# Two transformer blocks on one core: the router of the expert layer rebuilt, tokens gathered by pairs of experts in fp32, the output product finished block by block

## The chip, the cores and the metric

The kernel runs on one core of one Trainium2 chip. The metric is the device time of one execution in microseconds (us), as the median of several runs.

## The reference

256 tokens of width 1024 in fp32 go through two blocks. The first block has a mixer (gating over time beside a recurrence) and an expert layer, the second attention and a feed-forward part. The change lies at the end of the first block's mixer and in its expert layer:

```python
y = jnp.concatenate([y_a, y_b], axis=-1) @ w_out[l]          # the output product, 1024 x 1024
x = x + gate1[:, None, :] * y
h = _modulate(_rmsnorm(x, norm2_g[l]), shift2, scale2)
...
group_prob = jax.nn.softmax(ht @ rg_w + rg_b)                # 4 groups
g_p, g_idx = lax.top_k(group_prob, 1)
exp_logits = (ht @ re_w + re_b).reshape(N, 4, 8)             # 8 experts in each group
sel = jnp.take_along_axis(exp_logits, g_idx[:, :, None], axis=1)[:, 0]
e_p, e_idx = lax.top_k(jax.nn.softmax(sel, axis=-1), 2)
e_p = e_p / jnp.sum(e_p, axis=-1, keepdims=True)
weights = g_p * e_p
...
y_e = (silu(xb @ w_gate[e]) * (xb @ w_up[e])) @ w_down[e]    # for the tokens of each of 32 experts
```

Each token picks one group of four and two of its eight experts, whose results are added with their weights. The 32 experts have three matrices of 2 MiB each, 201 MB in all, and every one is read once. The shifts, scales and gates of a block come from a modulation, a product of one vector with a matrix of 1024 x 6144. The modulations of the second block do not depend on the first.

## The kernel before

**Order of work.** Most engines work in the order in which a scheduler places the instructions; inside `tc.manual_schedule` the order of the named engines is the order of the code. Loads are issued on SyncE's queue in the order of the code, and a load waits there until its buffer is free, with all that stand behind it.

**Output product** (`project_out`, from L845). For each of eight blocks of 128 weight rows the mixer's result is transposed and split in a high and a low part (`yh`, `yl`), the weight rows likewise by ACT (L167, `whi`) and VectorE (L168, `wlo`), in two buffers each. `mm3` (L416 to L418) then makes three products of 128x512 for each of two row tiles of tokens and two column halves, twelve per block, into four PSUM banks `pacc`. After the eighth block VectorE multiplies the four quarters by the gate and adds them to `x_sb`.

**Modulation** (L179 to L240). A vector of 1024 numbers takes four steps; a step loads 1 MiB, and makes eight small products per 128 rows (L190). The steps of the second block are used as filling: `fill(n)` places n of them, `need(...)` those that are still missing. `FILL_A[3]` = 8 steps stand ahead of the output product.

**Router** (from L948). Sixteen transposes of `x_sb` (L963), sixteen logit products of 36 columns (L971), the norm's factors, then the logits `L` for 4 groups and 32 experts. The group is chosen first (`first_max`: maximum, comparison, index, minimum, comparison), the eight logits of the chosen group are picked by multiplication and a sum (L1009), then the best and the second best of these, and their weights. `M` marks the two experts of a token. Products with a triangular matrix count the tokens of an expert ahead of each token, which gives its slot `pos`, and products with ones give the count of the fullest expert, `most`. The inputs for the experts are a scaled copy of `x_sb` as high and low part in fp32r: ACT writes `xh` (L1078) and `xf` (L1080), GpSimd `xl` (L1081).

**Experts** (L1187 to L1320). 16 pairs, in two groups (pairs 0 to 9 and 10 to 15), with PE's order by hand. `gather(quad)` compares slots with `pos` into a one-hot `D4` (L1190) and multiplies it with `xh` and `xl` (L1198): 32 products of 256 columns for four experts at 64 slots, copied to `xg` by ACT and VectorE in turn (L1202, L1204). `widen(j)` (L1216) makes the gate or the up product of a pair, 32 products of 512 columns, `narrow(j)` (L1261) the down product, `scatter(j)` (L1280, L1282) brings the results back to the tokens, with `x_sb` added after pair 12 (L1288). `places(j)` (L1240, L1245) turns the one-hot matrix. `turned(j)` transposes the hidden values. `bcast_cols` (L435) spreads a modulation vector over the partitions. Between the groups an `If` (L1120) treats experts with more than 64 tokens.

**Loads of the experts.** 192 loads of 1 MiB (`load_runs`, L149). The first 18 are issued ahead of the expert code, in the order `ORDER`, into buffers listed in `kept` (six of the ring shared with all loads of weights, `BIG` = 6 of the pool `bigp`, `MORE` = 2 of their own) and `EARLY` (buffers of tiles that are not in use yet). Each later one is issued when an earlier one's buffer is used up (`staged_moe`).

Of the kernel before, what the change touches and what calls it, by code (L numbers as in the profile page):

```python
# [20 lines left out]
D = 1024  # L21
# [38 lines left out]
def block(ctx, tc, A, out, dbg=None):  # L60
# [116 lines left out]
    on_dve = []  # L177

    def modulation(w, which, m, r0, each=False):  # L179
# [260 lines left out]
    with ExitStack() as c1:  # L440
# [404 lines left out]
        def project_out(kt):  # L845
# [16 lines left out]
            hi, lo = split_w(w_out[-1][:, kt % 2:kt % 2 + 1, :])  # L862
            for i in range(2):
                ts = slice(128 * i, 128 * i + 128)
                for n in range(2):
                    ns = slice(512 * n, 512 * n + 512)
                    mm3(op[i][n], (yh[:, kt, ts], yl[:, kt, ts]), (hi[:, 0, ns], lo[:, 0, ns]), kt == 0, kt == 7)
# [60 lines left out]
        for kt in range(4):  # L928
            project_out(kt)
# [6 lines left out]
        for kt in range(4, KT):  # L936
            project_out(kt)
        for i in range(2):
            for n in range(2):
                xs = x_sb[:, i, 512 * n:512 * n + 512]  # L940
                DVE.tensor_tensor(op[i][n], op[i][n], ga[:, n, :], op=OP.mult)
                DVE.tensor_tensor(xs, op[i][n], xs, op=OP.add)
        dump("x1", x_sb)


    with ExitStack() as c2:
        pool = c2.enter_context(tc.tile_pool(name="blk2", bufs=1, reuse_waits="tile"))
        G2 = pool.tile([128, 8], F32, name="G2")  # L948
        DVE.scalar_tensor_tensor(G2, modc[:, 4, :], 1.0, colr("n2g", 8), op0=OP.add, op1=OP.mult)
        big = lambda n: pool.tile([128, D], F32, name=n, tag="big", bufs=1)  # L950
        S2 = modc[:, 3, :]

# [6 lines left out]
        xT = pool.tile([128, KT, S], F32, name="xT", tag="xg", bufs=2)  # L959
        for kt in range(KT):  # L960
            p = pmm()
            for i in range(2):
                PE.transpose(p[:, 128 * i:128 * i + 128], x_sb[:, i, 128 * kt:128 * kt + 128], ident)  # L963
            if kt % 2:
                ACT.activation(xT[:, kt, :], p[:, 0:S], AF.Copy)
            else:
                DVE.tensor_copy(xT[:, kt, :], p[:, 0:S])
        pl = pmm()
        for i in range(2):
            for kt in range(KT):  # L970
                PE.matmul(pl[:, 64 * i:64 * i + 36], xT[:, kt, 128 * i:128 * i + 128], rw[:, kt, :],  # L971
                          start=i == 0 and kt == 0, stop=kt == KT - 1, skip_group_check=True)
        r = [rstd_x(i) for i in range(2)]
        need(5)
        need(6, 7)
        L = pool.tile([128, 2, 36], F32, name="L")
        for i in range(2):
            DVE.scalar_tensor_tensor(L[:, i, :], pl[:, 64 * i:64 * i + 36], r[i], rb, op0=OP.mult, op1=OP.add)


        t8 = lambda n, k=8: pool.tile([128, 2, k], F32, name="r_" + n)
        bb = lambda a, k: a.to_broadcast([128, 2, k])

        def first_max(v, k, n):

            m = t8(n + "m", 1)
            DVE.tensor_reduce(m, v, axis=AX.X, op=OP.max)
            c = t8(n + "c", k)
            DVE.tensor_tensor(c, v, bb(m, k), op=OP.is_equal)
            DVE.scalar_tensor_tensor(c, c, -64.0, io8[:, None, 0:k].to_broadcast([128, 2, k]), op0=OP.mult, op1=OP.add)  # L990
            f = t8(n + "f", 1)
            DVE.tensor_reduce(f, c, axis=AX.X, op=OP.min)
            o = t8(n + "o", k)
            DVE.tensor_tensor(o, c, bb(f, k), op=OP.is_equal)
            return m, o

        g4 = L[:, :, 0:4]
        gm_, og = first_max(g4, 4, "g")
        eg = t8("eg", 4)
        DVE.tensor_tensor(eg, g4, bb(gm_, 4), op=OP.subtract)  # L1000
        ACT.activation(eg, eg, AF.Exp)
        gs = t8("gs", 1)
        DVE.tensor_reduce(gs, eg, axis=AX.X, op=OP.add)
        pr = pool.tile([128, 2, 8, 4], F32, name="pr")
        for i in range(2):
            DVE.tensor_tensor(pr[:, i], L[:, i, 4:36].rearrange("p (g e) -> p e g", g=4),
                              og[:, i, None, :].to_broadcast([128, 8, 4]), op=OP.mult)
        sl8 = t8("sl8")
        DVE.tensor_reduce(sl8, pr, axis=AX.X, op=OP.add)  # L1009
        m1, o1 = first_max(sl8, 8, "a")  # L1010
        re8 = t8("re8")
        DVE.scalar_tensor_tensor(re8, o1, -1e30, sl8, op0=OP.mult, op1=OP.add)
        m2_, o2 = first_max(re8, 8, "b")
        e2 = t8("e2", 1)
        DVE.tensor_tensor(e2, m2_, m1, op=OP.subtract)
        ACT.activation(e2, e2, AF.Exp)
        w1, w2 = t8("w1", 1), t8("w2", 1)
        DVE.scalar_tensor_tensor(w1, e2, 1.0, gs, op0=OP.add, op1=OP.mult)
        DVE.reciprocal(w1, w1)
        DVE.tensor_tensor(w2, w1, e2, op=OP.mult)  # L1020
        M8, W8 = t8("M8"), t8("W8")
        DVE.tensor_tensor(M8, o1, o2, op=OP.add)
        DVE.tensor_tensor(o1, o1, bb(w1, 8), op=OP.mult)
        DVE.tensor_tensor(o2, o2, bb(w2, 8), op=OP.mult)
        DVE.tensor_tensor(W8, o1, o2, op=OP.add)
        M = pool.tile([128, 2, 32], F32, name="M")
        Wt = pool.tile([128, 2, 32], F32, name="Wt")
        for i in range(2):
            for dst, src in ((M, M8), (Wt, W8)):
                DVE.tensor_tensor(dst[:, i, :].rearrange("p (g e) -> p g e", g=4),  # L1030
                                  og[:, i, :, None].to_broadcast([128, 4, 8]),
                                  src[:, i, None, :].to_broadcast([128, 4, 8]), op=OP.mult)

        p = pmm()
        PE.matmul(p[:, 0:32], gt, M[:, 0, :], start=True, stop=True, skip_group_check=True)
        PE.matmul(p[:, 32:64], ones, M[:, 0, :], start=False, stop=False, skip_group_check=True)
        PE.matmul(p[:, 32:64], gt, M[:, 1, :], start=False, stop=True, skip_group_check=True)

        pc = pmm()
        PE.matmul(pc[:, 0:32], ones, M[:, 0, :], start=True, stop=False)  # L1040
# [68 lines left out]
        def crowded():  # L1109
# [10 lines left out]
            with tc.If(n_most > 64):  # L1120
                with tc.tile_pool(name="over", bufs=1) as op_, tc.For_i(0, 32) as e:
# [17 lines left out]
                    for b in range(2):  # L1139
                        bs = slice(128 * b, 128 * b + 128)  # L1140
                        p = pmm()
                        for i in range(2):
                            PE.matmul(p[:, 0:1], Do[:, i, bs].bitcast(F32), we_[:, i, :], start=i == 0, stop=i == 1)
# [610 lines left out]
```

## Time and profile before

| | us |
|---|---|
| median of 3 runs | 1443.49 (1443.27 to 1444.78) |
| the profiled execution's own time | 1445.49 |
| its span in the trace | 1443.7 |
| PE busy | 1356.1 (94%) |
| VectorE busy | 763.9 (53%) |
| ACT busy | 576.5 (40%) |
| GpSimd busy | 77.9 (5%) |

The DMA engines moved 400.42 MB, 277 GB/s in the mean. The page cuts the span in 40 slices of some 36 us:

```profile
PE   6999999699999988989979989999998999999997
...
PEclk9989999799999999999989999999999999999999
...
GB/s 361 295 69 251 164 274 380 226 365 426 426 427 426 427 427 402 391 426 427 427 246 252 196 228 146 336 276 311 286 248 181 172 117 149 184 196 196 178 150 30
```

Each digit is the busy share of PE in tenths, each PEclk digit TensorE's granted clock in tenths of full speed, the last line the DMA rate. Slice 7 (253 to 289 us, counted from 0) has the router: PE is busy for six tenths, at a clock of 0.7. The experts' loads fill slices 8 to 19. The busy shares are means over stages of different kinds; the rows further down are of single stretches and instructions.

### The profile page before, as it was taken

What the parts mean: (1) busy time and instruction counts of PE and PEld (TensorE: products, weight loads), DVE (VectorE), ACT (ScalarE), POOL (GpSimd) and SP (SyncE); (2) the same over time, 40 slices, a digit from 0 to 9 for tenths busy, and PEclk for the clock granted to TensorE, in tenths of its full rate; (3) what the DMA queues carried; (4) which work ended last, traced back from release to release, by engine and by line L of the source; (5) the groups of instructions that cost most, each with busy time, mean ns of one, the idle gap of its engine ahead of it and who ended that gap; (6) DMA issues with size and microseconds to landing.
All of it is one profiled execution on the core that took longest, in us unless ns stands there. A gap on an engine that the chain in (4) does not pass through costs nothing.

```text
span 1443.7 us, 22926 instructions
## 1 busy us (share of the span) xinstructions
PE 1356.1 (94%) x9330; PEld 1002.3 (69%) x9330; DVE 763.9 (53%) x1507; ACT 576.5 (40%) x1020; POOL 77.9 (5%) x79
## 2 busy tenths in 40 slices
PE   6999999699999988989979989999998999999997
PEld 5888878444444434534348867899996897799997
DVE  5648767511221111111165885888876575766565
ACT  3543013411111111101166755554456685654544
POOL 1002000100000000000020230000021001100000
PEclk9989999799999999999989999999999999999999
DMA  9826479599999999999967564988775534555540
GB/s 361 295 69 251 164 274 380 226 365 426 426 427 426 427 427 402 391 426 427 427 246 252 196 228 146 336 276 311 286 248 181 172 117 149 184 196 196 178 150 30
DMA packets 138688, 400.42 MB, mean 277 GB/s; under 512 B 6562, under 2 KB 84658, under 8 KB 114003
## 3 DMA queue, kind: packets, MB, share of 16 engines
q1 hardware_dynamic: 138578, 398.91, 72.0%
q8 instruction: 75, 1.23, 0.3%
q14 instruction: 35, 0.28, 0.1%
HBM read 397.82 MB, written 1.05 MB: 276 GB/s over the span
## 4 chain that ended last, share of the span: by engine, by line
PE 44%; DMA 9%; DVE 3%; ACT 3%; issue 1%; POOL 0%; POOLq 0%; DVEq 0%; SPq 0%; ACTq 0%
PE pmm L416 8%; PE pmm L417 8%; PE pmm L418 8%; PE pacc L416 5%; PE pacc L417 5%; PE pacc L418 5%; DMA wruns<-in_moe_w_gate_dram 4%; DMA wruns<-in_moe_w_down_dram 3%; DMA wruns<-in_moe_w_up_dram 2%; PE pmm L190 1%; PE pmm L1261 1%; ACT sqj L294 1%; PE pmm L366 1%; PE pmm L1622 1%; PE pmm L435 1%
## 5 line engine op out<-in xcount | busy, mean ns | idle before, releaser
L416 PE MATMUL pmm<-hh,whi 128*128 128x256 f32 (+1 forms) x1040 | 296.4, 285 | 2.0 <-ACT whi L167 2.0
L418 PE MATMUL pmm<-hh,wlo 128*128 128x256 f32 (+1 forms) x1040 | 297.1, 286 | 0.2 <-DVE wlo L168 0.2
L417 PE MATMUL pmm<-hl,whi 128*128 128x256 f32 (+1 forms) x1040 | 295.5, 284 | 0.0
L1216 PE MATMUL pmm<-wruns,xg 128*64 128x512 f32 x1024 | 233.1, 595 | 7.1 <-DMA wruns<-in_moe_w_gate_dram 7.1
L168 DVE TENSOR_TENSOR wlo<-wcols,whi 128x1024 fp32r<-128x1024 f32 (+1 forms) x130 | 168.4, 1300 | 99.3 <-ACT whi L167 98.8
L416 PEld LDWEIGHTS pmm<-hh,whi 128*128 128x128 f32 (+1 forms) x1040 | 197.6, 190 | 8.6 <-issue 3.6
L417 PEld LDWEIGHTS pmm<-hl,whi 128*128 128x128 f32 (+1 forms) x1040 | 196.6, 189 | 1.4
L418 PEld LDWEIGHTS pmm<-hh,wlo 128*128 128x128 f32 (+1 forms) x1040 | 197.0, 189 | 0.6 <-DVE wlo L168 0.4
L167 ACT ACTIVATE whi<-wcols 128x1024 fp32r<-128x1024 f32 (+1 forms) x130 | 136.1, 1053 | 119.0 <-PE pmm L417 91.7
L1216 PEld LDWEIGHTS pmm<-wruns,xg 128*64 128x64 f32 x1024 | 81.8, 137 | 141.1 <-issue 115.8
L168 DVE TENSOR_TENSOR wlo<-wrows,whi 128x1024 fp32r<-128x1024 f32 x87 | 108.1, 1248 | 56.3 <-ACT whi L167 55.9
L167 ACT ACTIVATE whi<-wrows 128x1024 fp32r<-128x1024 f32 x87 | 91.7, 1061 | 90.5 <-PE pmm L417 45.5
L1261 PE MATMUL pmm<-wruns,em 128*64 128x512 f32 x512 | 118.4, 595 | 7.2 <-DMA wruns<-in_moe_w_down_dram 5.7
L1261 PEld LDWEIGHTS pmm<-wruns,em 128*64 128x64 f32 x512 | 38.5, 137 | 79.3 <-issue 62.4
L1270 ACT ACTIVATE o<-ay 128x512 fp32r<-128x512 f32 x32 | 20.2, 631 | 177.5 <-DVE ay L1269 177.5
L1269 DVE SCALAR_TENSOR_TENSOR ay<-pmm,wsl,ga 128x512 f32<-128x512 f32 x32 | 24.0, 751 | 105.8 <-PE pmm L1261 103.8
L1307 DVE TENSOR_TENSOR ay<-ay,pmm 128x512 f32<-128x512 f32 x16 | 11.0, 688 | 120.0 <-PE pmm L1216 120.0
L1248 DVE COPY wsl<-pmm 64x1 f32<-64x1 f32 x32 | 5.0, 156 | 130.7 <-PE pmm L1245 130.4
L417 PE MATMUL pacc<-wlo,ah 128*128 128x512 f32 x176 | 69.2, 393 | 0.0
L416 PE MATMUL pacc<-whi,ah 128*128 128x512 f32 x176 | 68.9, 391 | 0.0
L418 PE MATMUL pacc<-whi,al 128*128 128x512 f32 x176 | 68.6, 393 | 0.0
L1222 ACT ACTIVATE ay<-pmm 128x512 f32<-128x512 f32 x16 | 9.6, 598 | 109.4 <-PE pmm L1216 109.4
(533 smaller groups left out, 2217.3 us busy)
## 6 DMA issues: line engine op xcount, KB each, us to landing
wruns<-in_moe_w_gate_dram SPq DMA_DIRECT2D x64, 1024.0 KB, 19.5
wruns<-in_moe_w_up_dram SPq DMA_DIRECT2D x64, 1024.0 KB, 19.5
wruns<-in_moe_w_down_dram SPq DMA_DIRECT2D x64, 1024.0 KB, 19.6
wrows<-in_w_mod_dram SPq DMA_DIRECT2D x48, 1024.0 KB, 7.0
wcols<-in_w_ffn_gate_dram SPq DMA_DIRECT2D x22, 1024.0 KB, 5.2
wcols<-in_w_ffn_up_dram SPq DMA_DIRECT2D x22, 1024.0 KB, 6.3
wrows<-in_w_ffn_down_dram SPq DMA_DIRECT2D x22, 1024.0 KB, 5.2
wrows<-in_ada_w_dram SPq DMA_DIRECT2D x16, 1024.0 KB, 7.7
```

Source lines behind the costliest of these rows:

```text
L167: ACT.activation(hi, src, AF.Copy)
L168: (POOL if ahead else DVE).tensor_tensor(lo, src, hi.bitcast(F32), op=OP.subtract)
L190: PE.matmul(p[32 * g:32 * g + 32, 0:n].rearrange("p (a j) -> p a j", j=32), lhsT, groups(rhs)[:, g], start=first, stop=last, skip_group_ch ...
L294: ACT.activation(j, src, AF.Square, accum_out=ss)
L366: PE.matmul(p, src[:, i, 128 * kt:128 * kt + 128], dg[i], start=True, stop=True)
L416: PE.matmul(p, a[0], b[0], start=first, stop=False, skip_group_check=True)
L417: PE.matmul(p, a[0], b[1], start=False, stop=False, skip_group_check=True)
L418: PE.matmul(p, a[1], b[0], start=False, stop=last, skip_group_check=True)
L1216: PE.matmul(p[64 * a:64 * a + 64, :], xg[:, kt, lc(2 * j + a)], wt[a][:, k, :], start=kt == 0, stop=kt == KT - 1, skip_group_check=True)
L1261: PE.matmul(pd[n][64 * a:64 * a + 64, :], hT[:, f, 64 * a:64 * a + 64], wt[a][:, b, 512 * n:512 * n + 512], start=f == 0, stop=f == 3, ski ...
L1269: DVE.scalar_tensor_tensor(yf, pd[n], wsl, ga2[:, ns], op0=OP.mult, op1=OP.mult)
L1270: ACT.activation(oh[:, ns], yf, AF.Copy)
```

## The change

- **Constants.** `MORE` 2 to 4; `ORDER` has load 18 in addition, `EARLY` no longer lends an `xg` buffer to load 12; `FILL_A[3]` 8 to 5.
- **Output product.** Blocks 0 to 5 as before. Blocks 6 and 7 are split first; then PE's, ACT's and VectorE's order is by hand: for each quarter (row tile, column half) the six products of both blocks, then its gate and sum, and for the first row tile the squares of the norm. Ahead of the last quarter PE transposes the first row tile (`turn_x`), four blocks into one PSUM bank. G2, the bias row `rb` and the scaling of `rw` move ahead of block 4.
- **Router.** PE's, VectorE's and ACT's order by hand. The logits of a row tile follow its transposes. Modulation steps stand at three places (`fill` 1, 2, 1), and in `hold` form: a vector's last three steps go into one PSUM bank and are added in one operation, after a further `yield`. The choice of best and second best is made in all four groups at once, on 8x8 elements per token partition (two row tiles by four groups), beside the group's choice; the product with the group's mark comes last. `M` is fp32r, and the products with it have fp32r copies of the triangle and of ones (`gtr`, `onr`). The weights `Wt` follow after the first one-hot matrix. The row factors for G2 and S2 are worked out ahead of the logits.
- **Gathering.** One scaled fp32 copy `xr` by ACT takes the place of `xh`, `xf` and `xl`; GpSimd's subtraction is gone. `gather(j)` is made for each pair instead of each second one: 16 fp32 products of 128 columns, into half of `xx`, the tile that held the transposes. It stands behind the up product of the pair before. `most` is worked out after the gathering for pair 1.

```diff
-MORE = 2
+MORE = 4
-EARLY = {4: "em", 3: "ay", 11: "oo", 12: "xg"}
-ORDER = (0, 1, 2, 5, 6, 7, 8, 9, 10, 3, 4, 11, 12, 13, 14, 15, 16, 17)
-FILL_A = (0, 0, 2, 8, 0, 2)
+EARLY = {4: "em", 3: "ay", 11: "oo"}
+ORDER = (0, 1, 2, 5, 6, 7, 8, 9, 10, 3, 4, 11, 12, 13, 14, 15, 16, 17, 18)
+FILL_A = (0, 0, 2, 5, 0, 2)
...
-                    p = gv[-1]()
+                    held = bool(hold) and q > 0
+                    if not held or q == 1:
+                        p = gv[-1]()
                     for kt in range(2 * q, 2 * q + 2):
-                        products(p, cb(kt), wt[:, kt % 2, :], kt == 2 * q, kt == 2 * q + 1)
-                    if q == 0:
+                        products(p, cb(kt), wt[:, kt % 2, :], kt == (2 if held else 2 * q), kt == (7 if held else 2 * q + 1))
+                    if held and q == 3:
+                        yield
+                    if held and q < 3:
+                        pass
+                    elif q == 0:
...
+        w = [project_out(kt) for kt in (6, 7)]
...
+        with tc.manual_schedule(engines={_E.PE, *MAN}):
+            for i in range(2):
+                for n, ns in enumerate(halves):
+                    for kt in (6, 7):
+                        project_on(kt, i, w[kt - 6], (n,))
+                    xs = x_sb[:, i, ns]
+                    DVE.tensor_tensor(op[i][n], op[i][n], ga[:, n, :], op=OP.mult)
+                    DVE.tensor_tensor(xs, op[i][n], xs, op=OP.add)
+                    if i == 0:
+                        rr[0].square(n, xs)
+                    if i == 1 and n == 0:
+                        turn_x(0, 0)
+                        turn_x(0, 1)
...
+            logits(0, 0)
+            r = [rr[0].end()]
+            logits(0, 1)
+            rr[1].first()
+            for g in range(2):
+                turn_x(1, g)
+            hold.append(True)
+            fill(1)
+            for g in range(2):
+                DVE.tensor_copy(xx[:, 1, 4 * g:4 * g + 4, :].rearrange("p k t -> p (k t)"), turned[1, g])
+                logits(1, g)
...
+            for i in range(2):
+                ACT.activation(xr[:, i, :].rearrange("t (k p) -> t k p", k=KT),
+                               x_sb[:, i, :].rearrange("t (p k) -> t k p", k=KT), AF.Copy, scale=r[i])
...
+            DVE.tensor_reduce(m1, el, axis=AX.X, op=OP.max)
+            DVE.tensor_reduce(gm_, gl, axis=AX.X, op=OP.max)
+            DVE.tensor_tensor(c8, el, on8(m1), op=OP.is_equal)
...
+            DVE.tensor_tensor(o2, c8, on8(f8), op=OP.is_equal)
+            DVE.tensor_tensor(c8, o1, o2, op=OP.add)
+            DVE.tensor_tensor(M.rearrange("p i (g e) -> p (i g) e", g=4), c8, on8(ogf), op=OP.mult)
+            p = pmm()
+            PE.matmul(p[:, 0:32], gtr, M[:, 0, :], start=True, stop=True, skip_group_check=True)
+            PE.matmul(p[:, 32:64], onr, M[:, 0, :], start=False, stop=False, skip_group_check=True)
+            PE.matmul(p[:, 32:64], gtr, M[:, 1, :], start=False, stop=True, skip_group_check=True)
+            DVE.scalar_tensor_tensor(pos, M.bitcast(F32), -1000.0, p[:, 0:64].rearrange("p (i e) -> p i e", i=2),
+                                     op0=OP.mult, op1=OP.add)
+            one_hot(D4, 0)
...
-            ACT.activation(xh[:, i, :].rearrange("t (k p) -> t k p", k=KT), xk, AF.Copy, scale=r[i])
-            xf = big("xf")
-            ACT.activation(xf.rearrange("t (k p) -> t k p", k=KT), xk, AF.Copy, scale=r[i])
-            POOL.tensor_tensor(xl[:, i, :], xf, xh[:, i, :].bitcast(F32), op=OP.subtract)
...
-                    for hx in (xh, xl):
-                        PE.matmul(p[:, 0:256], hx[:, i, 128 * kt:128 * kt + 128],
-                                  D4[:, i].rearrange("p e s -> p (e s)"), start=n == 0, stop=n == 3)
+                    PE.matmul(p[:, 0:128], xr[:, i, 128 * kt:128 * kt + 128],
+                              Dq[:, i, 2 * pr_:2 * pr_ + 2, :].rearrange("p e s -> p (e s)"), start=i == 0, stop=i == 1)
...
+                    if j is not None and j + 1 in g:
+                        gather(j + 1)
+                    if j == 0:
+                        most_()
                     if before is not None:
-                        if j is not None and j % 2 and j + 1 in g:
-                            gather((j + 1) // 2)
                         narrow(before)
```

## Rows read from the trace of the kernel before

**Rows 1.** stretches: length, us of PE, PEld, DVE, ACT, POOL, PEclk, DMA, GB/s

```profile
250.00:325.00 75.00, 63.22 (x341) 34.88 (x341) 27.46 (x86) 22.98 (x35) 4.70 (x2) 0.89 0.75 289
...
325.00:550.00 225.00, 215.18 (x1042) 92.50 (x1039) 41.50 (x80) 31.52 (x56) 0.00 (x0) 1.00 1.01 427
```

**Rows 2.** PE's timeline, two products that wait for loads (start, length, instruction, [idle <-releaser])

```profile
453.74 3.65 PE L1216 MATMUL pmm<-wruns,xg 128*64 128x512 f32 x14 [1.21 <-DMA wruns<-in_moe_w_gate_dram]
...
715.16 3.65 PE L1261 MATMUL pmm<-wruns,em 128*64 128x512 f32 x14 [1.14 <-DMA wruns<-in_moe_w_down_dram]
```

**Rows 3.** groups of PE, 203 to 223 us (count, busy us, mean ns)

```profile
L190 PE MATMUL pacc<-wrows,csil 128*32 128x256 f32 x78 | 6.0, 386 | 0.0
```

**Rows 4.** timelines of ACT, VectorE and PE, end of the output product

```profile
246.46 1.06 ACT L167 ACTIVATE whi<-wrows 128x1024 fp32r<-128x1024 f32 x1 [1.74 <-PE pacc L418]
...
247.55 1.22 DVE L168 TENSOR_TENSOR wlo<-wrows,whi 128x1024 fp32r<-128x1024 f32 x1 [1.58 <-ACT whi L167]
...
251.31 0.40 PE L417 MATMUL pacc<-wlo,yh 128*128 128x512 f32 x1
...
251.54 0.40 PE L418 MATMUL pacc<-whi,yl 128*128 128x512 f32 x1
...
255.24 1.23 PE L963 MATMUL pmm<-ident,x_sb 128*128 128x128 f32 x8 [0.26 <-ACT xT L965]
```

**Rows 5.** timeline of all engines, the router

```profile
256.36 3.76 PE L971 MATMUL pmm<-wfr,xT 128*128 128x36 f32 x32
...
261.93 2.36 POOL L1081 TENSOR_TENSOR xl<-xf,xh 128x1024 fp32r<-128x1024 f32 x1 [42.01 <-ACT xf L1080]
...
262.11 0.22 DVE L1009 TENSOR_REDUCE r_sl<-pr 128x16 f32<-128x64 f32 x1
...
262.57 1.75 DVE L989 TENSOR_TENSOR r_ac<-r_sl,r_am 128x16 f32<-128x16 f32 x1
...
266.58 2.31 DVE L1018 SCALAR_TENSOR_TENSOR r_w<-r_e,r_gs 128x2 f32<-128x2 f32 x1 [0.18 <-ACT r_e L1016]
...
273.02 0.55 PE L1198 MATMUL pmm<-D,xh 128*128 128x256 f32 x1 [0.75 <-DVE D L1190]
```

**Rows 6.** PE's timeline, first pairs of the experts

```profile
278.81 13.95 PE L1216 MATMUL pmm<-wruns,xg 128*64 128x512 f32 x64
...
292.69 2.05 PE L435 MATMUL pmm<-ident,modc 128*128 128x128 f32 x16
...
294.67 7.09 PE L1216 MATMUL pmm<-wruns,xg 128*64 128x512 f32 x32
...
313.87 7.09 PE L1261 MATMUL pmm<-wruns,em 128*64 128x512 f32 x32
...
361.52 0.39 PE L1198 MATMUL pmm<-D,xh 128*128 128x256 f32 x1
...
365.55 7.09 PE L1261 MATMUL pmm<-wruns,em 128*64 128x512 f32 x32
```

**Rows 7.** PE's timeline, end of the first group and the second

```profile
532.49 3.65 PE L1261 MATMUL pmm<-wruns,em 128*64 128x512 f32 x14 [1.25 <-DMA wruns<-in_moe_w_down_dram]
...
595.97 7.09 PE L1261 MATMUL pmm<-wruns,em 128*64 128x512 f32 x32
...
671.76 3.60 PE L1288 MATMUL pacc<-x_sb,ident 128*128 128x512 f32 x8
...
676.98 0.38 PE L1240 MATMUL pmm<-ident,D 128*128 128x128 f32 x2
```

**Rows 8.** waits of SyncE's queue, 216 to 330 us (total us, times, longest)

```profile
SPq L149 <- DVE pacc L941: 10.0, 1, 10.0
```

**Rows 9.** groups of PE's weight loads and products, 285 to 420 us

```profile
L1198 PEld LDWEIGHTS pmm<-D,xl 128*128 128x128 f32 x48 | 9.2, 191 | 0.0
...
L435 PEld LDWEIGHTS pmm<-ident,modc 128*128 128x128 f32 x16 | 1.9, 190 | 0.8 <-issue 0.8
...
L435 PE MATMUL pmm<-ident,modc 128*128 128x128 f32 x16 | 2.1, 281 | 0.0
```

More of the change, by code (lines that the diff above doesn't have):

```diff
@@ L177, in block @@
     on_dve = []
+    hold = []
     def modulation(w, which, m, r0, each=False):
@@ L935, in block @@
         need(3)
[L936 to L948, printed above, removed]
+        G2, S2 = G1, modc[:, 3, :]
         DVE.scalar_tensor_tensor(G2, modc[:, 4, :], 1.0, colr("n2g", 8), op0=OP.add, op1=OP.mult)
-        big = lambda n: pool.tile([128, D], F32, name=n, tag="big", bufs=1)
-        S2 = modc[:, 3, :]
         p = pmm()
@@ L968, in block @@
[L968 to L978, printed above, removed]
@@ L981, in block @@
[L981 to L995, printed above, removed]
@@ L997, in block @@
[L997 to L1007, printed above, removed]
@@ L1019, in block @@
[L1019 to L1032, printed above, removed]
@@ L1034, in block @@
[L1034 to L1040, printed above, removed]
-        PE.matmul(pc[:, 0:32], ones, M[:, 1, :], start=False, stop=True)
-        most = pool.tile([128, 1], F32, name="most")
@@ L1043, in block @@
-        DVE.tensor_reduce(most, pc[:, 0:32], axis=AX.X, op=OP.max)
-        mosti = pool.tile([128, 1], I32, name="mosti")
-        DVE.tensor_copy(mosti, most)
-        pos = pool.tile([128, 2, 32], F32, name="pos")
-        DVE.scalar_tensor_tensor(pos, M, -1000.0, p[:, 0:64].rearrange("p (i e) -> p i e", i=2), op0=OP.mult, op1=OP.add)
+        for kt in range(4, 6):
+            w = project_out(kt)
+            for i in range(2):
+                project_on(kt, i, w)
+        w = [project_out(kt) for kt in (6, 7)]
@@ new lines, in block, with turn_x @@
+        turned = {}
+        def turn_x(i, g):
+            p = turned[i, g] = pmm()
+            for k in range(4):
+                kt = 4 * g + k
+                PE.transpose(p[:, 128 * k:128 * k + 128], x_sb[:, i, 128 * kt:128 * kt + 128], ident)
+            return p
+        rr = [Rstd() for _ in range(2)]
+        halves = [slice(0, 512), slice(512, 1024)]
+        with tc.manual_schedule(engines={_E.PE, *MAN}):
+            for i in range(2):
+                for n, ns in enumerate(halves):
[9 more added lines that the diff above has]
+                        turn_x(0, 1)
+                if i == 0:
+                    rr[0].first()
+                    rr[0].second()
@@ L1172, in crowded, with most_ @@
                             for b in range(2):
-                                PE.matmul(p, Dt[:, b, 128 * i:128 * i + 128], yo[:, b, ns], start=b == 0, stop=b == 1)
+                                PE.matmul(p, Dt[:, b, 128 * i:128 * i + 128], yo[b][n], start=b == 0, stop=b == 1)
                             DVE.tensor_tensor(to, p, ga2[:, ns], op=OP.mult)
                             DVE.tensor_tensor(x_sb[:, i, ns], x_sb[:, i, ns], to, op=OP.add)
+        most = pool.tile([128, 1], F32, name="most")
+        mosti = pool.tile([128, 1], I32, name="mosti")
+        def most_():
+            p = pmm()
+            for i in range(2):
+                PE.matmul(p[:, 0:32], ones, M[:, i, :].bitcast(F32), start=i == 0, stop=i == 1)
+            DVE.tensor_reduce(most, p[:, 0:32], axis=AX.X, op=OP.max)
+            DVE.tensor_copy(mosti, most)
+        need(5, 6, 7)
         em = pool.tile([128, 4, 512], F32, name="em")
```

211 lines of the change are left out of this document (133 added, 78 removed).

## Prediction

> **What bounds the kernel now.** I read the profile by stages: busy time and DMA rate in stretches first, then PE's timeline through the expert stage, then the chain of the router.
>
> The table of stretches [rows 1] shows a kernel of two halves. From 325 to 550 us the DMA engines move 427 GB/s without a gap; a load of 1 MiB takes 1.0486 MB / 427 = 2.456 us, and the 192 loads of the experts 471.6 us. Between 250 and 325 the rate is 289: 75 x (1 - 289/427) = 24 us of DMA time are lost while the router decides and PE begins. It looks as if a shorter router and more buffers must give back a good part of these 24 us.
>
> PE's timeline says how far that goes [rows 2]. The first matmul of the experts that waits for a load stands at 453.74. Until then PE was late and the loads waited for buffers. From there on the loads are late, up to the 15th pair's down product, which waits for its last load at 715.16 and ends at 718.81. What follows 718.81 is not touched. So the question is when that product ends, and two paths lead to it: the queue of loads, and PE's own work since its first expert matmul, which I call W (278.81 now).
>
> **The change, part by part.** First the way to W.
>
> Three modulation steps leave the stretch ahead of the output product. There 78 of their matmul records keep PE busy 6.0 us [rows 3]; three steps are 48 records, 3.7 us at most. Part of them fills gaps in which the recurrence waits for VectorE anyway, so the gain is 0 to 3.7; I take 2.0.
>
> The output product is finished by quarters (row tile by column half): the six products of weight rows 6 and 7 for one quarter, then the next. The split halves of row 7 need the buffers of row 5, whose last product ends just before 246.46, where ACT begins on them; VectorE's half is done at 247.55 + 1.22 = 248.77 [rows 4]. Today the twelve products of row 6 (12 x (251.54 - 251.31) = 2.8 us) cover that. Blockwise only three stand ahead (0.7 us): the fifth product waits for the low half, 2.3 - 0.7 = 1.6 us. If the halves come sooner it is 0, at worst 2.3. Eight transposes of the first row tile come in ahead of the last quarter, eight matmul records with 1.23 us in a row today [rows 4]: 1.0 to 1.2; I take 1.0, since their tail overlaps. So the last output product ends at 251.94 - 2.0 + 1.6 + 1.0 = 252.5.
>
> From there to the first gathering product it is 273.02 - (251.54 + 0.40) = 21.1 us now [rows 4, 5]. Afterwards PE's order is fixed by hand. Eight logit products of the first row tile: sixteen take 3.76 [rows 5], so 1.9. Eight transposes of the second: 1.0. One modulation step: 16 records, 1.0. Eight logit products: 1.9. That is 5.8. VectorE's passes over the last quarter and its copies of the transposes lie beside it. Two small products, the copy of their result and four operations that form the logits (some 0.2 each, as the reduction below): 7.4. The choice on 64 elements has 13 operations that depend on one another; a reduction of 64 elements takes 0.22 [rows 5], with the gap 0.25 to 0.26, and the other six slip in between: 3.6, so 11.1. Then three one-pass products, the slot numbers, the one-hot comparison: 1.9. That makes 13.0, 8.1 us less than now. Of these, 3.6 are sure: two VectorE operations on 16 and 2 elements took 1.75 and 2.31 us, longer than the 0.22 of 64 elements; the first ended at 264.32, with GpSimd's subtraction (261.93 + 2.36 = 264.29, [rows 5]), the second likewise. GpSimd has no such work any more. Its queue keeps two iotas.
>
> The first gathering takes 278.81 - 273.02 = 5.8 now [rows 5, 6]. Afterwards it is 16 fp32 products of 128 columns. Today's nearest rows are eight fp32 products of 128 columns between 292.69 and 294.67: 0.2475 each. [...] W becomes 252.5 + 13.0 + 5.5 = 271.0, 7.8 us sooner, with bounds of 268 (full 3.7 us, no wait for row 7) and 274.2 (nothing in front, a wait of 2.3, the lower clock throughout).
>
> Now the work behind W, where the change adds. Two pairs without a wait take 365.55 - 313.87 = 51.68 us, of which one gathering of four experts 365.55 - 361.52 = 4.03 [rows 6]: 23.83 per pair without it. Afterwards each pair has a gathering of 16 x 0.2475 = 3.96 of its own in place of 2.01: 27.8 a pair, still under the 12 x 2.456 = 29.5 of its loads. But a head start must be kept up for ten pairs, and here it is used up.
> - W to the first down product: 313.87 - 278.81 = 35.06 now, plus one more gathering and the two products of the fullest expert's count (0.47): 39.5.
> - Eight pairs to the ninth down product, seven gatherings: 8 x 23.83 + 7 x 3.96 = 218.4; the product itself 7.1.
> - From its end, 532.49 + 3.65 = 536.14 now, over the branch between the groups to the second group's first down product, 595.97 [rows 7]: 59.8, plus one gathering more: 63.8.
> - Four pairs, three gatherings, and 676.98 - 671.76 = 5.2 for what the scatter of pair 12 adds [rows 7]: 95.3 + 11.9 + 5.2 = 112.4; then 7.1.
>
> The sum is W + 448.3 = 719.3, against 718.81 today. PE becomes the bound of the whole stage, and the 7.8 us won are spent: 15 gatherings of 3.96 stand on this path in place of seven of 4.03, 31 us more, which take up the waits for loads since 453 and the head start.
>
> Edits put at nothing: two more buffers and 19 loads ahead instead of 18 let the queue lead by 4.9 us more, but no one waits for it. ACT writes one scaled copy per row tile instead of two, beside the 13.0. The three moved modulation loads go on SyncE's queue behind the output weights, and hold three of the six ring buffers until their products in the router. Expert loads 9, 10 and 12 need these buffers, and a load that waits holds all behind it, as one did for 10.0 us [rows 8]. At worst the queue stands until the second moved step ends, 252.5 + 7.3 = 259.8, with eight loads landed. With some 4 us for the next to land and 5 for a pause at the branch, both allowances, the 188th lands at 263.8 + 179 x 2.456 + 5 = 708.4, and its product could end at 712.1, 7 us ahead of PE. That wait costs nothing either.
>
> [...] The weight loads of the gathering from fp32r took 191 ns, those of an fp32 product 190 [rows 9]: no difference. [...]
>
> **Forecast.** The profiled execution took 1445.49 us, 1.8 outside its span and 2.0 above the median of 1443.49. The change adds 719.3 - 718.8 = 0.5: 1444.0 us. A difference under 0.2%, 2.9 us, can't be told from none.
>
> **Rivals.**
> - Faster: the loads stay the bound. The pair of 27.8 us is shorter than its loads' 29.5, which speaks for it; that PE waits for nothing until 453 speaks against. At W = 268 and 0.235 a product (the logits' pace, [rows 5]) the end comes 3.0 + 240 x 0.0125 = 6.0 sooner: 1438. If the added products cost nothing at all, the queue sets the end, ahead by two buffers (4.9) and the 7.8 us of W: 1443.5 - 12.7 = 1431. Chance 0.32.
> - Slower: the gathering products don't overlap. An fp32 product of 128 columns has a mean length of 0.281 of its own [rows 9]; at that pace the 240 products between W and the 15th pair cost 240 x 0.0335 = 8.0 us more, 1452. It decides from 0.2475 + 2.4/240 = 0.258 on. Four PSUM banks, emptied in turn by two engines, could bring it about; against it, eight in a row ran at 0.2475. With a W of 274 alone it would be 1447. Chance 0.30, of which 0.01 for the rule on weight loads.
> - The change doesn't do what it says: the router's tiles lie where the first block's were, and a copy waits for their last reader, so that the first row tile isn't ahead of the second. That is 2 us on W, 1446, and no more; it belongs with no change.
>
> **Numbers.** No change 0.38, faster 0.32, slower 0.30. The range runs from 1436, between the two faster ends, to 1450.5, just short of the full price of the slower one.
>
> **What would show it.** The first expert matmul near 271, PE's order before it without the 9 us of idle. Gathering products 0.24 to 0.25 apart, 4 us each pair. Hardly a wait of PE for a load before the second group's end, and gaps in the DMA rate at the end of the first. The 15th pair's down product ending near 719. The forecast is wrong if waits for loads remain from 450 on (then faster), or if W comes after 274 or a pair without waits takes over 28.5 (then slower).

## The result and the profile after

The changed kernel takes 1457.17 us (median of 4 runs, 1453.3 to 1458.22), the kernel before 1443.93 in the same session: a ratio of 1.0086, 95% interval 1.0066 to 1.0107. It is slower by 13.2 us in the medians, where 0.5 us was forecast; the range ended at 1450.5. The profiled execution took 1456.29 us, its span is 1454.5.

The stretches of the changed kernel, with 225 to 250 us in front, answer to [rows 1] (length, us of PE, PEld, VectorE, ACT, GpSimd, PEclk, DMA share, GB/s):

```profile
225.00:250.00 25.00, 22.43 (x115) 17.89 (x115) 16.55 (x39) 9.49 (x14) 0.22 (x2) 1.00 0.37 131
...
250.00:325.00 75.00, 71.82 (x443) 40.49 (x442) 25.25 (x92) 21.22 (x41) 0.00 (x0) 0.98 0.96 396
325.00:550.00 225.00, 222.35 (x1156) 103.03 (x1155) 46.59 (x96) 36.85 (x72) 0.00 (x0) 1.00 1.01 426
```

The stretch of the router and the first experts looks as one would wish: 396 GB/s against 289, a clock of 0.98 against 0.89, PE busy 71.8 of 75 us. But the loads that are won there were lost ahead of it: from 225 to 250 us the rate is 131. PE's timeline answers to [rows 4 to 7]:

```profile
254.35 0.39 PE L425 MATMUL pacc<-whi,yl 128*128 128x512 f32 x1
...
264.86 0.25 PE L1116 MATMUL pmm<-M,gor 128*128 128x32 f32 x1 [2.31 <-DVE M L1113]
...
266.21 5.52 PE L1262 MATMUL pmm<-D,xr 128*128 128x128 f32 x32 [0.86 <-DVE D L1018]
...
271.65 13.95 PE L1279 MATMUL pmm<-wruns,xx 128*64 128x512 f32 x64
...
310.41 7.09 PE L1323 MATMUL pmm<-wruns,em 128*64 128x512 f32 x32
...
334.32 3.84 PE L1262 MATMUL pmm<-D,xr 128*128 128x128 f32 x32
...
338.09 7.09 PE L1323 MATMUL pmm<-wruns,em 128*64 128x512 f32 x32
...
528.03 7.04 PE L1323 MATMUL pmm<-wruns,em 128*64 128x512 f32 x32
...
556.33 0.77 PE L1262 MATMUL pmm<-D,xr 128*128 128x128 f32 x2 [5.69 <-PEq L1174]
...
561.70 6.05 PE L1262 MATMUL pmm<-D,xr 128*128 128x128 f32 x30 [4.61 <-issue]
...
567.69 13.95 PE L1279 MATMUL pmm<-wruns,xx 128*64 128x512 f32 x64
...
604.29 7.09 PE L1323 MATMUL pmm<-wruns,em 128*64 128x512 f32 x32
...
716.39 7.04 PE L1323 MATMUL pmm<-wruns,em 128*64 128x512 f32 x32
```

The first expert matmul stands at 271.65 (before 278.81). From there no product of the experts waits for a load, where the kernel before waits from 453.74 on [rows 2]: PE sets the pace. The 15th pair's down product (716.39) ends at 723.43, against 718.81. On the way lies one thing that was not there before: behind the branch between the groups PE makes one gathering product (two matmul records), stands still for 4.61 us with nothing that the profile shows as a cause, and then makes the other fifteen in 6.05 us. The kernel before has one wait of PE from 552 to 568 us, the one at the branch, and its products behind the branch follow one another (total us, times, longest):

```profile
PE pmm L1198 <- PEq L1120: 5.9, 1, 5.9
```

From 723.43 to the end it is 1454.5 - 723.43 = 731.1 us; in the kernel before 1443.7 - 718.81 = 724.9. So 4.6 us are lost up to the 15th pair and 6.2 behind it, where the change, by its diff, touches nothing. PE's waits in the second half of the changed kernel (total us, times, longest) show two that the kernel before has not:

```profile
PE pmm L191 <- DVE gm L224: 10.1, 1, 10.1
...
PE pmm L191 <- DMA wrows<-in_w_mod_dram: 2.4, 1, 2.4
```

Line 191 is the product of a modulation step.

### The profile page after: what moved, and what is told of

Read it like the earlier page. It is cut to its first block, busy times and chain, and to the rows that moved or that the text cites. A ratio compares the mean times of both kernels' runs of the same rounds, so it can differ in the third digit from the quotient of the medians.

```text
span 1454.5 us, 23499 instructions
## 1 busy us (share of the span) xinstructions
PE 1375.8 (95%) x9583; PEld 1018.0 (70%) x9583; DVE 765.2 (53%) x1526; ACT 583.4 (40%) x1052; POOL 73.3 (5%) x77
## 4 chain that ended last, share of the span: by engine, by line
PE 54%; DVE 3%; ACT 2%; issue 1%; DMA 0%; POOL 0%; DVEq 0%; ACTq 0%
PE pmm L424 8%; PE pmm L423 8%; PE pmm L425 8%; PE pmm L1279 6%; PE pacc L423 5%; PE pacc L424 5%; PE pacc L425 5%; PE pmm L1323 3%; PE pmm L1262 2%; PE pmm L191 1%; PE pmm L442 1%; PE pmm L373 1%; DVE wlo L168 1%; ACT whi L167 1%; ACT sqj L301 0%
## 5 line engine op out<-in xcount | busy, mean ns | idle before, releaser
L1279 PE MATMUL pmm<-wruns,xx 128*64 128x512 f32 x1024 | 225.7, 594 | 0.0
L1279 PEld LDWEIGHTS pmm<-wruns,xx 128*64 128x64 f32 x1024 | 71.9, 137 | 136.5 <-issue 134.8
L1323 PE MATMUL pmm<-wruns,em 128*64 128x512 f32 x512 | 113.3, 595 | 1.4 <-ACT em L1295 1.4
L1266 ACT ACTIVATE xx<-pmm,GS 128x128 f32<-128x128 f32 x64 | 29.3, 458 | 143.5 <-PE pmm L1262 143.5
L1323 PEld LDWEIGHTS pmm<-wruns,em 128*64 128x64 f32 x512 | 35.5, 137 | 68.4 <-issue 64.2
L1262 PEld LDWEIGHTS pmm<-D,xr 128*128 128x128 f32 x512 | 62.8, 203 | 22.5 <-issue 22.5
L1262 PE MATMUL pmm<-D,xr 128*128 128x128 f32 x512 | 66.0, 290 | 11.2 <-PEq L1174 5.7
L424 PE MATMUL pacc<-wlo,ah 128*128 128x512 f32 x176 | 69.2, 393 | 0.0
```

Source lines behind the costliest of these rows:

```text
L424: PE.matmul(p, a[0], b[1], start=False, stop=False, skip_group_check=True)
L1262: PE.matmul(p[:, 0:128], xr[:, i, 128 * kt:128 * kt + 128], Dq[:, i, 2 * pr_:2 * pr_ + 2, :].rearrange("p e s -> p (e s)"), start=i == 0, ...
L1266: ACT.activation(xg, p[:, 0:128], AF.Identity, scale=G2r[:, kt:kt + 1], bias=S2r[:, kt:kt + 1])
L1279: PE.matmul(p[64 * a:64 * a + 64, :], xg[:, kt, 64 * a:64 * a + 64], wt[a][:, k, :], start=kt == 0, stop=kt == KT - 1, skip_group_check=True)
L1323: PE.matmul(pd[n][64 * a:64 * a + 64, :], hT[:, f, 64 * a:64 * a + 64], wt[a][:, b, 512 * n:512 * n + 512], start=f == 0, stop=f == 3, ski ...
```

## The experiments

In the diffs the code is that of the changed kernel, if not said otherwise. `hold` is the list that switches the held form of a modulation on; the change appends to it in the router and never clears it.

### The held form ended, and the shift alone

```diff
+        hold.clear()
         dump("pos", pos)
```

> The changed kernel, with its held form of modulation (one more yield for each vector) switched off behind the router. Theory: the held form stays on in the second block, where every vector then takes five steps of filling instead of four, so that the counts written for four leave later vectors behind; PE waits 10.1 us for a modulation sum at the second layer's start, and 2.4 us for a load ahead of the first feed-forward part. With it switched off the steps of the second block stand where they stood before, what follows the experts is as long as before, 6.2 us shorter: 1451 us, 7 above the kernel before, and the 10.1 us wait is gone. Rival: the longer second half comes from the loads or the clock that the expert stage leaves behind; then nothing changes, 1457 us.

Measured: 1452.87 us, ratio 1.0063 (1.0047 to 1.0079). The wait of 10.1 us is gone, and the part behind the 15th pair takes 1449.7 - 722.83 = 726.9 us. That is 4.2 of the 6.2 us in this trace; in the seven traces further down it takes 724.9 to 725.8 us, near the 724.9 of the kernel before.

The second run puts that one step into the kernel before:

```diff
+                if late_ and not dve and q == 3:
+                    yield
                 if q < 3:
                     yield
...
         need(5)
         need(6, 7)
+        late_.append(True)
```

> The kernel before, with nothing of the change but one more yield per modulation vector from the router on, so that the steps of the second block stand as in the changed kernel. Theory of the shifted filling: the expert stage stays as it is, up to 718.8 us, and what follows gets 6 us longer, 1449 to 1450 us. Rival (the second half is longer for another reason): 1443.5 us, within 1.5.

Measured: 1457.45 us, ratio 1.0080 (1.0063 to 1.0097). Two rows of its PE timeline, the 15th pair's down product and the product that waits:

```profile
716.66 3.65 PE L1265 MATMUL pmm<-wruns,em 128*64 128x512 f32 x14 [1.15 <-DMA wruns<-in_moe_w_down_dram]
...
1108.29 1.08 PE L191 MATMUL pmm<-gm,ones 128*32 128x256 f32 x8 [10.10 <-DVE gm L224]
```

The expert stage ends at 716.66 + 3.65 = 720.3 and what follows takes 1456.5 - 720.3 = 736.2 us, 11.3 more than before: the direction of the theory, with more than its size. Why the shift costs 11.3 us here and 6.2 in the changed kernel stays open. How it comes about can be counted from the code and seen in the waits. Fillings are given in counts (`FILL`), set for four steps per vector. With five, each count of the second block ends earlier in the work. At the first layer's feed-forward part three steps of a vector are missing, not one, and `need` puts them in front of the norm, with a wait for their loads (2.4 us in the changed kernel). At the second layer's start VectorE still has the last two additions of a vector's sum to make, 2.60 us together, in a stretch whose order is by hand; PE's product for it stands ahead of the work of the norm and waits 10.1 us, and all of PE's queue with it.

### The branch between the groups

```diff
                 scatter(g[-1])
+                if g[0] == 0:
+                    p = pmm()
+                    for n in range(8):
+                        PE.matmul(p[:, 0:8], ident, ident[:, 0:8], start=True, stop=True)
             if g[0] == 0:
                 crowded()
```

(with the held form ended)

> As the run with the held form switched off, and eight small matmuls of no use stand on PE at the end of the first group, ahead of the branch, where PE waits for the branch anyway. They move the code behind the branch to another place. Theory: the 4.6 us in which PE stands still after two gathering products behind the branch, with nothing that it waits for, are the loading of its next instructions; at another place in the code the stop goes or moves to another product, and if it goes, the second group starts 5 to 6 us earlier and the time falls by 4 to 6 us, to about 1446 us. Rival: the stop belongs to the fp32 gathering itself; it stays at the same product and the time is the same within 1 us.

Measured: 1446.88 us, ratio 1.0014 (1.0002 to 1.0026). PE's timeline of the run without padding, and then of the run with it:

```profile
555.98 0.77 PE L1263 MATMUL pmm<-D,xr 128*128 128x128 f32 x2 [5.79 <-PEq L1175]
...
561.18 5.99 PE L1263 MATMUL pmm<-D,xr 128*128 128x128 f32 x30 [4.43 <-issue]
...
715.79 7.04 PE L1324 MATMUL pmm<-wruns,em 128*64 128x512 f32 x32
```

```profile
272.62 12.67 PE L1280 MATMUL pmm<-wruns,xx 128*64 128x512 f32 x58
...
551.45 1.84 PE L1387 MATMUL pmm<-ident 128*128 128x8 f32 x16
...
557.81 5.32 PE L1263 MATMUL pmm<-D,xr 128*128 128x128 f32 x32 [4.51 <-PEq L1175]
...
711.75 7.04 PE L1324 MATMUL pmm<-wruns,em 128*64 128x512 f32 x32
```

The stop is gone, the 32 records follow one another, and the 15th pair ends at 718.79 us, 4.0 sooner. Matmuls that compute nothing made the kernel 6 us faster. The next run leaves PE's path as it was and moves the code alone, by work in the body of the branch, which is not run:

```diff
                     with ...For_i(0, 32) as e:
+                    pu = pmm()
+                    for _ in range(57):
+                        PE.matmul(pu[:, 0:8], ident, ident[:, 0:8], start=True, stop=True)
```

> As the run with the held form ended, without padding on PE's path; 57 small matmuls stand in the body of the branch, which is not run, so that PE's code behind the branch lies 228 instructions further on, and nothing else differs. In the run beside it PE stopped for 4.4 us after one gathering product behind the branch. [...] Rival 1 (the stop belongs to the gathering): it stays after one product and lasts 4.4 us. [...]

Measured: 1446.57 us, ratio 1.0018 (1.0006 to 1.0031).

```profile
556.31 3.54 PE L1266 MATMUL pmm<-D,xr 128*128 128x128 f32 x15 [5.68 <-PEq L1175]
...
561.51 2.06 PE L1266 MATMUL pmm<-D,xr 128*128 128x128 f32 x17 [1.66 <-issue]
...
563.50 7.09 PE L1283 MATMUL pmm<-wruns,xx 128*64 128x512 f32 x32
```

The stop is now after 15 records, and lasts 1.66 us. What has not moved is the time at which PE goes on: 561.51 - 556.31 = 5.20 us after the first product, 5.37 and 5.20 in the two traces with the early stop. So the gathering isn't what stops: the stop hangs on where the code lies, and it ends 5.2 to 5.4 us after PE began behind the branch. That PE has no instructions left there and gets the next ones at that time is the author's reading; one thing in the trace of the changed kernel speaks for it. Among the DMA queues the profile lists some of the kind `instruction`. One of them has no packet from 556 to 559 us and one from 559 to 562 us (queue, kind: packets, MB, share of 16 engines):

```profile
q8 instruction: 1, 0.02, 2.1%
```

In windows of 0.1 us this packet lies between 559.2 and 559.3 us, and PE goes on at 561.70, 2.4 to 2.5 us later. The kernel before has one between 560.6 and 560.7 us, and no stop: its products follow one another from 557.60 us on.

Rival 1 is refuted. At which places of the code a stop can come no run shows; that it would come later in the gathering, and be shorter, was the author's estimate. The time is 6.3 us below the 1452.87 of the run with the held form ended: the 17 records behind the stop take 2.06 us, 0.12 each, as in a gathering at a granted clock of 1.00 (3.77 us for 32, from 334.32 us in the changed kernel), against 5.99 us for 30, 0.20 each, and the second group's first expert matmul stands at 563.50, against 567.69 in the changed kernel.

### What the gatherings cost

```diff
                     if j is not None and j + 1 in g:
-                        gather(j + 1)
+                        gather(j + 1, (j + 1) % 2 == 0)
```

(with the held form ended; `gather` makes its products only where the second argument is true)

> As the run with the held form switched off, and the gatherings of the odd pairs are left out (their experts work on other columns), so that seven to eight gatherings of 3.77 us are missing ahead of the 15th pair's down product. Theory: PE is the bound of the expert stage and the loads stand some 5 us behind it as the next bound; 30 us of PE work go, PE waits for loads again, and the end comes 4 to 9 us earlier than in the run beside it: 1443 to 1447 us. Rival (the gatherings cost nothing, the loads or the branch between the groups set the end): within 1.5 us of the run beside it.

Measured: 1441.59 us, ratio 0.9976 (0.9964 to 0.9989), below the range expected.

```profile
558.16 6.22 PE L1263 MATMUL pmm<-D,xr 128*128 128x128 f32 x32 [5.78 <-PEq L1175]
...
714.33 3.65 PE L1324 MATMUL pmm<-wruns,em 128*64 128x512 f32 x14 [1.14 <-DMA wruns<-in_moe_w_down_dram]
```

PE waits for loads again, and the 15th pair ends at 717.98. Here the code lies elsewhere and there is no stop, so the run to compare is that with padding: 718.79 in its trace, 1446.88 in its median. Eight gatherings of 3.77 us, 30 us of PE work, are worth 0.8 us at the end of the stage in the traces (whose own times are 1444.88 and 1445.96) and 5.3 in the medians: less than a fifth of them. The first expert matmul of this run stands at 274.90, 2.3 us later than in the run with padding, so the 0.8 us may be too little. The loads stand 0.8 to 5.3 us behind PE, where the theory had some 5.

### The steps in the router and the gathering by fours

From here on the padding of the branch stays, and the held form, where it is used, ends with the router. First the three modulation steps go back ahead of the output product:

```diff
-FILL_A = (0, 0, 2, 5, 0, 2)
+FILL_A = (0, 0, 2, 8, 0, 2)
...
-            hold.append(True)
-            fill(1)
...
-            fill(2)
...
-            fill(1)
-        hold.clear()
```

> As the run with the eight small matmuls ahead of the branch (held form ended, 1446.9 us, the 15th pair's down product ending at 718.8 us), but the three modulation steps stand ahead of the output product again, as before the change, and none in the router. Their loads then no longer hold three ring buffers and the queue until 262 us, so that the loads of the experts come sooner. Theory: PE sets the end of the expert stage, and its own work starts 1 to 3 us later with the steps in front: 0 to 3 us more, 1447 to 1450 us. Rival: the queue that stands still from 222 to 262 us is what costs time; then the loads gain 6 us or more and the time falls by over 1.5 us, below 1445.

Measured: 1443.7 us, ratio 0.9988 (0.9976 to 1.0001). The rival's time, but not its reason:

```profile
222.19 0.50 PE L423 MATMUL pacc<-whi,yh 128*128 128x512 f32 x1
...
264.97 5.40 PE L1258 MATMUL pmm<-D,xr 128*128 128x128 f32 x32 [0.86 <-DVE D L1018]
...
270.30 13.95 PE L1275 MATMUL pmm<-wruns,xx 128*64 128x512 f32 x64
...
709.39 7.04 PE L1319 MATMUL pmm<-wruns,em 128*64 128x512 f32 x32
```

The first expert matmul comes at 270.30 (272.62 in the run beside it, 271.2 to 274.9 in five traces with the steps in the router), the pair ends at 716.43, and PE waits for no load in either run. From the first expert matmul to the end of the 15th pair it is 446.2 us in the run beside it and 446.1 here. The loads were not what was gained; PE's start was. The rate from 225 to 250 us is 383 GB/s instead of 113, and buys nothing as long as PE is the bound.

Then the gathering of the kernel before:

```diff
-MORE = 4
+MORE = 2
...
-                PE.matmul(p[:, 0:128], xr..., Dq[...], start=i == 0, stop=i == 1)
+                for hx in (xh, xl):
+                    PE.matmul(p[:, 0:256], hx[:, i, 128 * kt:128 * kt + 128], D4[:, i]..., ...)
...
+            for i in range(2):
+                DVE.scalar_tensor_tensor(xl[:, i, :]..., x_sb[:, i, :]..., r[i], xh[:, i, :]..., op0=OP.mult,
+                                         op1=OP.subtract)
```

> As the run with the steps ahead, and the gathering is that of the kernel before: high and low part in fp32r, four experts at once, two added buffers and not four; the low part is made by VectorE from the scaled tokens in one operation, and not by GpSimd. The new router, the blockwise output product and the branch's padding stay. Theory: PE has 28 us less work behind its first expert matmul, so the loads are the bound again; the faster router frees their buffers 4 to 7 us sooner, and the 15th pair ends at 712 to 715 us: 1437 to 1441 us, below both kernels. Rival: the low part on VectorE and the first gathering take back what the router won (first expert matmul at 276 us or later), and the loads come no sooner: 1443 to 1446 us.

Measured: 1442.06 us, ratio 0.9980 (0.9967 to 0.9993), between the range of the theory and that of the rival. The interval ends below 1, but the difference to the kernel before, 2.4 us, is no more than the 0.2% that the prediction calls no change.

```profile
269.12 1.86 PE L1267 MATMUL pmm<-D,xl 128*128 128x256 f32 x7 [1.38 <-DVE xl L1121]
...
274.51 10.76 PE L1296 MATMUL pmm<-wruns,xg 128*64 128x512 f32 x48
...
711.63 3.65 PE L1341 MATMUL pmm<-wruns,em 128*64 128x512 f32 x14 [1.15 <-DMA wruns<-in_moe_w_down_dram]
```

The loads are the bound and the 15th pair ends at 715.28. The low part on VectorE costs a wait of 1.38 us and the start is 4 us later than with the steps ahead alone. Its median is still the lowest of the versions that do all the work, 1.6 us below that of the run with the steps ahead, whose executions spread over 6 us.

> The run with quads, but with the three modulation steps in the router, as the change has them, and the held form ended behind it: against the run with the padded branch (1446.9 us) only the gathering is undone. Theory: PE no longer sets the end; the loads do, which stood at most 1 us behind it when half of the gatherings were left out (718.0 us against 718.8), because their queue is held until 262 us: 1444 to 1447 us, and 3 us or more above the run with quads and the steps ahead. Rival: the held loads cost nothing; then both runs with quads are within 1.5 us.

(its edit is the one before, with the steps in the router as the change has them)

Measured: 1445.75 us, ratio 1.0007 (0.9993 to 1.0020).

```profile
274.28 0.80 PE L1272 MATMUL pmm<-D,xh 128*128 128x256 f32 x2 [4.80 <-DVE ga L239]
...
279.35 6.23 PE L1301 MATMUL pmm<-wruns,xg 128*64 128x512 f32 x28
...
716.09 3.65 PE L1346 MATMUL pmm<-wruns,em 128*64 128x512 f32 x14 [1.14 <-DMA wruns<-in_moe_w_down_dram]
```

It is 3.7 us above the run before, with quads and the steps ahead, as expected, but the trace does not settle that the queue is why. A new wait of 4.80 us stands in the first gathering: its products need a PSUM bank that the held modulation sum still occupies, and VectorE comes to that sum (L239) only after the low parts. The first expert matmul is 4.8 us later, and the loads end 4.5 us later. Which of the two, the late start or the queue (130 GB/s from 225 to 250 us), sets the loads' end stays open.

> A try for a version that beats both: as the run with quads and the steps ahead, but the first four experts are gathered by pairs in fp32 from one scaled copy, as in the change, and the high and low parts for the later quads are made from that copy while the first pairs are worked on; one load fewer is issued ahead. Theory: the first expert matmul comes at 270 to 271 us as in the run with the steps ahead (274.5 with quads from the start), the buffers come free 4 us sooner, and the loads, which stay the bound, end 2 to 4 us sooner than the 715.3 us there: 1438 to 1440 us. Rival: the buffer given up for the scaled copy (2.5 us of loading) and the extra gathering take it back: 1441 to 1444 us.

```diff
-                gather(g[0])
+                gather(g[0] // 2) if g[0] else gather_pair(0)
...
                     if j == 0:
+                        gather_pair(1)
                         most_()
```

(with a scaled fp32 copy `xr` in the second buffer of the gathered tokens, and one load fewer in `ORDER`)

Measured: 1444.8 us, ratio 1.0003 (0.9992 to 1.0015).

```profile
271.30 13.95 PE L1303 MATMUL pmm<-wruns,xx 128*64 128x512 f32 x64
...
711.31 3.65 PE L1348 MATMUL pmm<-wruns,em 128*64 128x512 f32 x14 [1.15 <-DMA wruns<-in_moe_w_down_dram]
```

PE starts 3.2 us sooner and the loads end 0.3 us sooner: the rival. The rate from 250 to 325 us is 293 GB/s, against 307 in the run with quads, which is one load or 2.5 us of loading less; that the given-up buffer is why is the rival's reading, and not shown by itself.

## Why the prediction was wrong, step by step

**"What follows 718.81 is not touched."** This step failed, by 6.2 us. The diff was read for the modulation's form in the router, and not for its state: a list that is appended to and never cleared changes the number of steps of every later vector, and the counts of filling in the second block hang on that number. Without it what follows takes 725 to 727 us, with it 731, and 736 in the kernel before with the shift alone.

**"From its end ... over the branch ...: 59.8, plus one gathering more: 63.8."** This step failed, by 5.4 us: from 528.03 + 7.04 = 535.07 to 604.29 it is 69.2. The stretch was taken over from the trace of before, where PE does not stop behind the branch, as if it would stay so wherever the code lies. In the changed kernel a stop of 4.61 us came in there, and the products behind it took 6.05 us, at a granted clock of 0.50 up to 566 us. Where the padding takes the stop away the stretch is 63.6 us (529.00 + 7.04 = 536.04 to 599.66), as forecast. With both side effects gone the 15th pair ends at 718.8, half a microsecond from the 719.3 of the sum, and the kernel at a ratio of 1.0014, inside the 0.2% called no change, though its interval (1.0002 to 1.0026) reaches past it. So small a miss is luck in part: W is 272.62 in that run, 1.6 us later than forecast, and what follows W 2.1 us shorter.

**The rest of the sum held.** W was 271.65 for a forecast of 271.0; W to the first down product 38.8 (39.5); eight pairs 217.6 (218.4); the last four 112.1 (112.4). A gathering takes 338.09 - 334.32 = 3.77 us, 0.236 a product (0.2475), and a pair 27.7 (27.8). The groups from 285 to 420 us answer to [rows 9]:

```profile
L1262 PE MATMUL pmm<-D,xr 128*128 128x128 f32 x183 | 21.9, 278 | 0.0
...
L1262 PEld LDWEIGHTS pmm<-D,xr 128*128 128x128 f32 x184 | 21.0, 192 | 4.1 <-issue 4.1
```

The mean length of 278 ns is there, as for the products of [rows 9], but the products overlap: the slower rival, by its mechanism, did not come true, although its sign did. The weight loads, to which that rival gives 0.01 of its chance, take 192 ns, as those of fp32r did before (191 ns, [rows 9]).

**W was right by terms that cancel.** The three steps taken from in front of the output product were to give 2.0 us; its first product stands at 222.86 with five steps and at 222.19 with eight (the run with the steps ahead). Other traces have it from 220.6 to 224.2 with five and from 219.3 to 224.1 with eight, so that a gain of 2.0 us is not shown. PE waited 1.27 us for the halves of row 7 (1.6 taken), and 1.27 for `yh` of block 4 at 240.65, which the prediction did not have. The last output product ended at 254.74, not 252.5; from there the router took 11.5 us, not 13.0. No run shows what the 5.5 us are made of that the sum has for the first gathering; in the changed kernel it took 271.65 - 266.21 = 5.44 us, at a granted clock of 0.50 from 267 to 269 us and of 1.00 from 270 us on.

**"Edits put at nothing."** The load behind the second moved step was issued at 261.75, where 259.8 was taken as the worst. Of the queue's waits on the way two end with products of the moved steps, 5.9 us together; the longest ends with VectorE's split of the mixer's result (SyncE's queue from 216 to 330 us, total, times, longest):

```profile
SPq L149 <- DVE yl L866: 10.3, 1, 10.3
...
SPq L149 <- PE pmm L191: 5.9, 2, 3.0
```

With PE as the bound that costs nothing, as the run with the steps ahead shows: PE had no waits for loads before, and none after. What the steps in the router cost is PE's start, 2.3 us in these two traces and 3.2 in the medians. But the loads were not 7 us ahead of PE, as the 712.1 had it: where they set the end again, with half of the gatherings, the 15th pair ends at 717.98.

**Where the gain went.** The router saved 7.2 us, as forecast within 0.7, and the gatherings by pairs took it back, as forecast; with half of them left out the loads set the end, 1 to 5 us sooner. Of the loss of 13 us some 10 come from two side effects: a list that stayed filled (1457.17 to 1452.87) and the place of some code (1452.87 to 1446.88). The rest is the size of what the steps in the router cost (1446.88 to 1443.70).

## What to carry to other kernels

Where work is spread by counts of a generator's steps, a change of the steps moves all later work; print the order of the instructions behind the change and compare it with the order of before, however far from the edit. Behind a branch that is taken at run time, look for a stop with no releaser (here 4.61 us) and for a packet of the instruction queue ahead of its end (here 2.4 to 2.5 us), and try whether some idle instructions ahead of the branch, or code moved within it, make it go. A faster start is worth nothing where the next bound stands as close behind as the loads did here: leave the suspected work out in one run before rebuilding it.

## What of the hardware was not expected

In the five traces with a stop behind the branch PE made a few products there and went on 5.1 to 5.4 us after the first of them (561.70 - 556.33 = 5.37 in the changed kernel, where the DMA engines moved 424 GB/s meanwhile). In between it stood still: 4.6 and 4.4 us after one product, 1.7 us after seven and a half. The two runs with quads have a stop too, after 16 products of 256 columns, so it is not bound to the fp32 gathering (1.62 us at 564.48 with the steps in the router; with the steps ahead):

```profile
559.85 0.40 PE L1267 MATMUL pmm<-D,xh 128*128 128x256 f32 x2 [1.35 <-issue]
```

The kernel before, the run with padding and that with the steps ahead and the gathering by pairs make their whole gathering there without a gap. The stretches of the changed kernel, and then two of the kernel before (columns as above), show the granted clock beside it:

```profile
555.00:560.00 5.00, 0.77 (x2) 0.50 (x2) 0.76 (x2) 0.00 (x0) 0.00 (x0) 0.50 1.01 424
560.00:565.00 5.00, 3.30 (x15) 3.30 (x16) 0.82 (x2) 0.46 (x1) 0.00 (x0) 0.50 1.01 423
```

```profile
555.00:560.00 5.00, 2.40 (x11) 2.43 (x12) 1.31 (x3) 0.26 (x1) 0.00 (x0) 0.50 1.00 419
560.00:565.00 5.00, 5.00 (x33) 4.12 (x33) 1.63 (x3) 2.00 (x4) 0.00 (x0) 0.96 1.01 421
```

The granted clock is 0.50 in both kernels from 554 us on, while PE waits at the branch, so the stop is not what brought it there. But in the kernel before it is back at 1.00 from 561 us on, and in the changed kernel only from 567 us on: it is still 0.50 from 562 to 565 us, when PE is busy again. The sixteen gathering products take 3.77 us at a granted clock of 1.00 (from 334.32 us in the changed kernel), 5.32 us behind the branch in the run with padding, and 0.77 + 6.05 us beside the stop in the changed kernel.
